# One merge-gate block placed earlier, three recurrence outputs placed before the scores, and one half-row add moved to GpSimd

## The chip, the cores and the metric

The kernel runs on one core of a Trainium2 chip. The metric is the device time in microseconds of one launch; for a kernel before and after a change, the medians of several runs are compared. All data is fp32. Where a matrix product is made, both operands are split into a high part in the type `float32r` and a low rest, and three products (high by high, low by high, high by low) are added up in PSUM, the accumulation memory of TensorE.

## The reference

One decoder layer over 512 tokens of width 1024. The input is normalised and projected once into ten pieces; two branches (block-sparse attention with 8 heads of 64, and a gated linear recurrence with 4 heads of 128) run beside each other; each is gated, projected up, and the two are merged by sigmoid gates; then come an output projection, a residual, and a gated input embedding.

```
xn = rmsnorm(h, norm_gain)
aq, ak, av, ag, bq, bf, bi, bg, gate_a, gate_b = split(xn @ w_in)
ya = moba_attention(rmsnorm(aq), rmsnorm(ak), av, rel_bias)      # 8 heads x 64
ya = (ya * silu(ag)) @ w_up_a
yb = hgrn2_chunkwise(silu(bq), kb(bf), bi, log_f(bf))            # 4 heads x 128
yb = (rmsnorm(yb) * silu(bg)) @ w_up_b
merged = sigmoid(gate_a) * ya + sigmoid(gate_b) * yb
h = h + merged @ w_out
h = h + (p @ w_ple) * sigmoid(h @ w_ple_gate)
```

## The kernel before

Everything after the first stage lies with features on the 128 partitions and the 512 tokens along the free axis. A dense block is one piece of 128 output features: 8 steps over the 1024 inputs, 3 matmuls of 128x512 in each, 24 in all, accumulated in one PSUM bank (`mm3`, L289 to L295). Banks come from three pools: `mm` with 3 (dense blocks, the fourth score bank of a run and the attention outputs), `a` with 3 (scores and recurrence outputs), `g` with 2 (diagonal blocks and states of the recurrence).

The order of TensorE is written out by hand. The main line goes through the list `ORDER` (L54 to L56): `bg` and `ag` are the output gates of recurrence and attention (`silu_block`, L486: three ScalarE instructions and a VectorE multiply, L491, that reads the bank last), `bf` stands for a head's forget and query blocks, `ga` and `gb` for the merge gates (`sigmoid`, L297: three ScalarE instructions, of which only the first reads the bank), `ub` for the recurrence's up-projection. Then follow the attention's up-projection (`ua`), the output projection (`h`, L1163) and the gated embedding (L1193 to L1279, product L1210, embedding `pe`).

Attention and recurrence are generators that are fed in between by a clock in the source: `mm3` and its kin call `tick` after each step of 3 matmuls, which adds the step's assumed time (0.681 us) to `now` and lets every generator run that is due; `cost` adds time without letting anybody run. What they issue on TensorE stands there, in that order, for good. The orders of VectorE and ScalarE and of the DMA queues are made by a planner from a simulated timeline, with the order of the source as priority; `high_priority` blocks go ahead. SyncE's queue (SP) issues most transfers, GpSimd's (POOL) the weights.

The attention (`attention`, L788) takes the head pairs 0 to 3 in two runs each: run 0 has the query blocks 0, 1, 2 and run 1 the query block 3 (`STEPS`). For each run it issues the scores on TensorE (L815), the bias, maximum, exponential and scaling (L832 to L836), transposes on VectorE (L839), and 16 transfers on SP that put the turned probabilities in their place (L850). The products with the values (`o`, L863) of a pair come behind the scores of the next pair's run 0; their last two fifths use run 1. After the scores of a run the generator sleeps for `PACE[run]`; of the sleep that ends in a run 0, the last 8 us (`BIAS`) begin with the transfers of the next bias (L880).

The recurrence (`hgrn_intra`, L529) makes decay products for a head, waits until the attention has issued its next run (`beside_attention`), and then puts small diagonal matmuls (`lpb`, `lpa`, L592 to L611) on TensorE. The output products of the head before (`hop`, L676 to L680, `cost(1.5)`) lie as a function in the list `hops` until then, and are issued in front of those matmuls (L583). Head 3's come by a clock of their own.

The end: for each of four pairs of output rows there are products in the gate, the embedding, and `merge` (L1181): sigmoid, multiply by the embedding (L1189), add of the residual (L1190, on VectorE where `n % 4 == 3`, on GpSimd elsewhere), and the store (L1191). Row 3 comes last, and its left half in two pieces of 128 tokens: `pe3l` and then `pe3m`.

Of the kernel before, what the change touches and what calls it, by code (L numbers as in the profile page):

```python
# [15 lines left out]
OP = mybir.AluOpType  # L16
# [12 lines left out]
LEVELS = (16, 8, 4, 2, 1)  # L29

STEPS = ((0, 1, 2), (3,))
PACE = (19.5, 22.5)

HP = 2.5
H0 = 8.0
# [16 lines left out]
XN = (0.6,) * 7 + (2.0, 0.6)  # L52

ORDER = [("bg", 0), ("ag", 0), ("bf", 1), ("bg", 1), ("ag", 1), ("gb", 0), ("bf", 2), ("gb", 1), ("gb", 2), ("bg", 2), ("ag", 2),  # L54
         ("gb", 3), ("bf", 3), ("gb", 4), ("gb", 5), ("bg", 3), ("ag", 3), ("ga", 0), ("ga", 1), ("gb", 6), ("gb", 7),
         ("ga", 4), ("ga", 2), ("ga", 3), ("ga", 5), ("ga", 6), ("ga", 7)] + [("ub", i) for i in range(KD)]  # L56

PAIRED = [n // 2 + 4 * (n % 2) for n in range(KD)]
# [10 lines left out]
def hybrid_layer_kernel(  # L69
# [17 lines left out]
    V, A, G, PE = nc.vector, nc.scalar, nc.gpsimd, nc.tensor  # L87
# [14 lines left out]
    def bank(tag, name):  # L102
        return psum.tile([128, 512], F32, tag=tag, bufs={"mm": 3, "g": 2, "a": 3}[tag], name=name)
# [34 lines left out]
    def cost(us):  # L138
        now[0] += us
# [18 lines left out]
    def held_from(us, insts, until=None):  # L158

        def later():  # L160
            for inst in insts if until not in done else []:
                held(inst)
            yield 0.0

        spawn(later(), us)
# [331 lines left out]
    hops = []  # L497
# [290 lines left out]
    def attention(qn, kn, va, sags, res):  # L788
        def place(qb, j):

            return {0: (j, 0), 1: (2, 256 * j), 2: (j, 128), 3: (j, 0)}[qb]

        def tiles(step):
            return 2 + (len(STEPS[step]) > 1)
# [3 lines left out]
        def scores(hp, step):  # L798
            (qh, ql), (kh, kl) = qn[hp], kn[hp]
            nt = tiles(step)  # L800

            sps = [bank("a", f"s{hp}{step}{i}") for i in range(nt)]
            extra = bank("mm", f"s{hp}{step}x") if nt > 2 else None

            def where(qb, j):
                b_, o = place(qb, j)
                return (extra, 0) if (qb, j) == (1, 1) else (sps[b_], o)

            for qb in STEPS[step]:
                nk = 128 * (qb + 1)  # L810
                for i in range(3):
                    for j in range(2):
                        js = slice(64 * j, 64 * j + 64)
                        b_, o = where(qb, j)
                        PE.matmul(b_[:, o:o + nk], (qh, ql, qh)[i][js, qb * 128:qb * 128 + 128], (kh, kh, kl)[i][js, :nk],  # L815
                                  start=(i == 0), stop=(i == 2))
            cost(sum(3 * max(0.107, (qb + 1) * 0.0538) for qb in STEPS[step]))
            return where

        def softmax(hp, step, T, where):  # L820

            nt = tiles(step)
            z = pb[:, Z0[step]:Z0[step] + nt].rearrange("p t f -> p (t f)").rearrange("p (b t f) -> p b t f", b=4, t=nt)
            with tc.high_priority(offset=AHEAD):
                left = [sum(place(qb, j)[0] == b for qb in STEPS[step] for j in range(2)) for b in range(nt)]
                for qb, j in [(qb, j) for qb in STEPS[step] for j in range(2)]:
                    b_, o = place(qb, j)
                    nk = 128 * (qb + 1)
                    p_ = pb[:, b_, o:o + nk]
                    st = unit("ps", f"ps{hp}{qb}{j}", shape=(128, 4))  # L830
                    s_, so = where(qb, j)
                    in_order(V.tensor_tensor_reduce(p_, s_[:, so:so + nk], T[j][:, nk - 1::-1], -1.0, 3e38,  # L832
                                                    OP.add, OP.min, st[:, 0:1]))
                    A.activation(p_, p_, AF.Exp, bias=st[:, 0:1], scale=-1.0, accum_out=st[:, 1:2])  # L834
                    V.reciprocal(st[:, 2:3], st[:, 1:2])
                    A.activation(p_, p_, AF.Copy, scale=st[:, 2:3])  # L836
                    left[b_] -= 1
                    if left[b_] == 0:
                        V.transpose(z[:, :, b_, :].rearrange("p b (n c) -> p b n c", c=32),  # L839
                                    pb[:, b_].rearrange("p (n b c) -> p b n c", b=4, c=32))  # L840
            return z

        def sorted_groups(step, z):

            nt = tiles(step)
            pt = pb[:, PT0[step]:PT0[step] + nt].rearrange("p t f -> p (t f)").rearrange("p (a t f) -> p a t f", a=4, t=nt)
            with tc.high_priority(offset=AHEAD):
                for a in range(4):
                    for b in range(4):
                        nc.sync.dma_start(pt[32 * b:32 * b + 32, a], z[32 * a:32 * a + 32, b])  # L850
            return pt.rearrange("p a t (n c) -> p a (t n) c", c=32)

        def out_values(hp, pts):

            o = bank("mm", f"o{hp}")
            for step, pt in enumerate(pts):
                for qb in STEPS[step]:
                    qs = slice(qb * 128, qb * 128 + 128)
                    for kb in range(qb + 1):
                        for j in range(2):  # L860
                            h0 = hp * 128 + 64 * j
                            b_, o0 = place(qb, j)
                            PE.matmul(o[64 * j:64 * j + 64, qs], va[kb][:, h0:h0 + 64], pt[:, :, 4 * b_ + o0 // 128 + kb, :],  # L863
                                      start=(kb == 0), stop=(kb == qb))
            cost(1.5)
            sag = sags[hp]
            V.tensor_tensor(sag, o, sag, op=OP.mult)
            h_ = unit("A", f"yah{hp}", R)
            l_ = unit("A", f"yal{hp}", R)
            split(h_, l_, sag)  # L870
            res.append((h_, l_))
            done.add(f"ya{hp}")
# [3 lines left out]
        def bias(hp):  # L876
            for j in range(2):
                t = unit("T", f"bias{hp}{j}")
                row = ed[2 * hp + j:2 * hp + j + 1, :]
                held(nc.sync.dma_start(t, bass.AP(tensor=row.tensor, offset=row.offset, ap=[[1, 128], [1, 512]])))  # L880
                T[hp, j] = t
# [10 lines left out]
        for n in range(len(steps) + 1):  # L892
            ahead = BIAS if 0 < n < len(steps) and steps[n][1] == 0 else 0.0
            if n >= 1:
                yield PACE[steps[n - 1][1]] - ahead
            if ahead:
                bias(steps[n][0])
                yield ahead
            if n < len(steps):
                hp, i = steps[n]  # L900
                where = scores(hp, i)
            if n >= 1 and steps[n - 1][1] == NS - 1:
                ho = steps[n - 1][0]
                while f"ag{ho}" not in done:
                    yield lambda: f"ag{ho}" in done
                out_values(ho, [pts.pop(n - NS + i_) for i_ in range(NS)])
            if n < len(steps):
                z = softmax(hp, i, [T[hp, 0], T[hp, 1]], where)
                if others:
                    parts.clear()  # L910
                    others.pop()()
                    for n_, p_ in enumerate(list(parts)):
                        held_from(16.0 + 2.0 * n_, [p_])
                pts[n] = sorted_groups(i, z)
            runs[0] += 1
# [84 lines left out]
    spawn(qk_norm("q", proj_tok(0, "aq", xh, xl), qgain[:, 0:1], qn))  # L1000
    spawn(qk_norm("k", proj_tok(1, "ak", xh, xl), kgain, kn))
    spawn(attention(qn, kn, va, sags, ya))
    def up(i, n, ys, name):
        ws = weight(w_up[n, i])
# [22 lines left out]
    for n in range(KD):  # L1027
        ga, gb = sg["ga", n], sg["gb", n]
# [11 lines left out]
    hf, xt, wt, edge = {}, {}, {}, []  # L1040
# [140 lines left out]
    def merge(n, c, ps, pes, t, plus=None):  # L1181
        if plus is not None:
            with tc.high_priority(offset=AHEAD):
                V.tensor_tensor(t[:, c], ps, plus, op=OP.add)  # L1184
            ps = t[:, c]
        if ps is not None:
            A.activation(t[:, c], ps, AF.Sigmoid)  # L1187
        yield
        V.tensor_tensor(t[:, c], t[:, c], pes()[:, c], op=OP.mult)  # L1189
        (V if n % 4 == 3 else G).tensor_tensor(t[:, c], t[:, c], hf[n][:, c], op=OP.add)  # L1190
        nc.sync.dma_start(out[n][:, c], t[:, c])  # L1191

    for p in range(4):  # L1193
# [152 lines left out]
```

## Time and profile before

| what | value |
|---|---|
| median of 3 runs | 451.46 us |
| lowest, highest | 451.43, 453.24 us |
| the profiled execution | 452.42 us |
| its span, first to last instruction | 450.6 us |
| granted TensorE clock, mean | 0.999 |
| DMA | 59.53 MB, mean 132 GB/s |

The profile comes from one execution, whose own time is 452.42 us: 1.8 us of that lie outside of the span. Times in the trace are microseconds from the start of the span. Engines are PE (TensorE matmuls), PEld (its weight loads), DVE (VectorE), ACT (ScalarE), POOL (GpSimd) and SP (SyncE); a small q marks an engine's queue of issued transfers. "[0.40 <-DVE bg3s L491]" behind a row means that the engine was idle for 0.40 us before it and that the instruction of line 491 which wrote `bg3s` ended the wait.

### The profile page before, as it was taken

What the parts mean: (1) busy time and instruction counts of PE and PEld (TensorE: products, weight loads), DVE (VectorE), ACT (ScalarE), POOL (GpSimd) and SP (SyncE); (2) the same over time, 40 slices, a digit from 0 to 9 for tenths busy, and PEclk for the clock granted to TensorE, in tenths of its full rate; (3) what the DMA queues carried; (4) which work ended last, traced back from release to release, by engine and by line L of the source; (5) the groups of instructions that cost most, each with busy time, mean ns of one, the idle gap of its engine ahead of it and who ended that gap; (6) DMA issues with size and microseconds to landing.
All of it is one profiled execution on the core that took longest, in us unless ns stands there. A gap on an engine that the chain in (4) does not pass through costs nothing.

```text
span 450.6 us, 8536 instructions
## 1 busy us (share of the span) xinstructions
PE 445.8 (99%) x3192; PEld 376.2 (83%) x3192; DVE 334.6 (74%) x682; ACT 289.7 (64%) x561; POOL 59.9 (13%) x97
## 2 busy tenths in 40 slices
PE   9999999999999999999999999999999999999996
PEld 8888888888878888878887888878888888899996
DVE  5869494776899797949857775465479868999844
ACT  5958474746689988979857996784135434555421
POOL 1000100000000101010100000111210103325520
PEclk9999999999999999999999999999999999999999
DMA  8802424168594455171425444265551444312111
GB/s 265 317 1 94 141 93 129 48 219 197 167 215 127 159 134 178 46 203 49 142 93 155 140 135 148 70 197 149 184 173 47 168 145 143 129 47 95 49 47 48
DMA packets 32857, 59.53 MB, mean 132 GB/s; under 512 B 7088, under 2 KB 18736, under 8 KB 32816
## 3 DMA queue, kind: packets, MB, share of 16 engines
q0 software_dynamic: 9056, 32.51, 22.5%
q1 hardware_dynamic: 23616, 26.47, 20.4%
q8 instruction: 25, 0.41, 0.4%
q14 instruction: 16, 0.13, 0.1%
q10 hardware_dynamic: 144, 0.01, 0.0%
HBM read 48.74 MB, written 4.98 MB: 119 GB/s over the span
## 4 chain that ended last, share of the span: by engine, by line
PE 89%; DVE 5%; SPq 2%; DMA 1%; issue 1%; ACT 0%; DVEq 0%
PE h L293 10%; PE g L1210 9%; PE ga L293 9%; PE gb L293 7%; PE ub L293 5%; PE aq L423 5%; PE ak L423 5%; PE ua L293 5%; PE av L423 5%; PE bf L293 5%; PE bi L423 5%; PE bq L293 4%; PE bg L293 4%; PE ag L293 4%; PE pe L293 2%; SPq L850 2%
## 5 line engine op out<-in xcount | busy, mean ns | idle before, releaser
L276 ACT ACTIVATE wh<-wf 128x1024 fp32r<-128x1024 f32 (+1 forms) x70 | 67.0, 958 | 63.2 <-issue 9.8
L277 DVE TENSOR_TENSOR wl<-wf,wh 128x1024 fp32r<-128x1024 f32 (+1 forms) x70 | 76.8, 1097 | 38.0 <-ACT wh L276 35.7
L266 POOL DMA_DIRECT2D wf<-in_w_tr_dram x30 | 15.8, 528 | 170.5 <-DVE wl L277 115.4
L293 PE MATMUL ga<-xh,wh 128*128 128x512 f32 x64 | 25.3, 396 | 0.4 <-DVE bg3s L491 0.4
L293 PE MATMUL gb<-xh,wh 128*128 128x512 f32 x64 | 25.0, 391 | 0.0
L293 PE MATMUL ga<-xh,wl 128*128 128x512 f32 x64 | 24.9, 390 | 0.0
L293 PE MATMUL ga<-xl,wh 128*128 128x512 f32 x64 | 24.9, 389 | 0.0
L293 PE MATMUL gb<-xl,wh 128*128 128x512 f32 x64 | 24.9, 389 | 0.0
L293 PE MATMUL h<-mh,wh 128*128 128x512 f32 x64 | 24.9, 389 | 0.0
L293 PE MATMUL h<-ml,wh 128*128 128x512 f32 x64 | 24.9, 389 | 0.0
L293 PE MATMUL h<-mh,wl 128*128 128x512 f32 x64 | 24.9, 389 | 0.0
L293 PE MATMUL gb<-xh,wl 128*128 128x512 f32 x64 | 24.9, 389 | 0.0
L834 ACT ACTIVATE pb<-pb,ps 128x128 f32<-128x128 f32 (+3 forms) x32 | 17.6, 551 | 10.0 <-DVE ps L832 10.0
L832 DVE CUSTOM_DVE_ANT_0 pb<-s,bias 128x128 f32<-128x128 f32 (+3 forms) x28 | 12.8, 493 | 7.1 <-DMA bias<-in_ed_dram 4.8
L1187 ACT ACTIVATE sg<-sg 128x256 f32<-128x256 f32 x12 | 5.0, 414 | 20.2 <-DVE sg L1184 20.2
L836 ACT ACTIVATE pb<-pb,ps 128x128 f32<-128x128 f32 (+3 forms) x32 | 16.0, 550 | 0.0
L542 ACT ACTIVATE hx<-hx 128x512 f32<-128x512 f32 x24 | 14.9, 623 | 1.4 <-DVE hx L541 1.3
L266 POOL DMA_DIRECT2D wf<-in_w_up_dram x16 | 8.6, 538 | 52.2 <-DVE wl L277 32.2
L839 DVE STREAM_TRANSPOSE pb<-pb 128x512 f32<-128x512 f32 x20 | 13.8, 696 | 2.0 <-ACT pb L836 2.0
L266 POOL DMA_DIRECT2D wf<-in_w_tok_dram x8 | 4.4, 549 | 80.2 <-DVE wl L277 68.2
L293 PEld LDWEIGHTS ga<-xh,wh 128*128 128x128 f32 x64 | 12.0, 188 | 3.5 <-DVE bg3s L491 0.8
L293 PEld LDWEIGHTS ga<-xh,wl 128*128 128x128 f32 x64 | 12.0, 188 | 2.6
(958 smaller groups left out, 1434.9 us busy)
## 6 DMA issues: line engine op xcount, KB each, us to landing
wf<-in_w_tr_dram POOLq DMA_DIRECT2D x30, 512.0 KB, 4.2
wf<-in_w_tok_dram POOLq DMA_DIRECT2D x8, 512.0 KB, 3.6
wf<-in_w_up_dram POOLq DMA_DIRECT2D x16, 256.0 KB, 3.0
wf<-in_w_o_dram POOLq DMA_DIRECT2D x8, 512.0 KB, 3.8
wf<-in_w_g_dram POOLq DMA_DIRECT2D x8, 512.0 KB, 3.6
wf<-in_w_tok_dram SPq DMA_DIRECT2D x6, 512.0 KB, 7.6
pb<-pb SPq DMA_DIRECT2D x64, 48.0 KB, 2.9
bias<-in_ed_dram SPq DMA_DIRECT2D x8, 256.0 KB, 4.1
```

What stands on the lines that cost most here:

```text
L266: (G if len(wraw) >= FAR else nc.sync).dma_start(raw, ap)
L276: rounds[i] = A.activation(hi, wraw[i], AF.Copy)
L277: V.tensor_tensor(lo, wraw[i], hi.bitcast(F32), op=OP.subtract)
L293: dense.append(PE.matmul(ps, a[:, k, :], b[k], start=(n == 0), stop=(n == tot - 1)))
L423: dense.append(PE.matmul(banks[t], a[:, s_], b[:, kk, :], start=(k == 0 and i == 0), stop=(k == KD - 1 and i == 2)))
L542: A.activation(x, x, AF.Exp)
L832: in_order(V.tensor_tensor_reduce(p_, s_[:, so:so + nk], T[j][:, nk - 1::-1], -1.0, 3e38, OP.add, OP.min, st[:, 0:1]))
L834: A.activation(p_, p_, AF.Exp, bias=st[:, 0:1], scale=-1.0, accum_out=st[:, 1:2])
L836: A.activation(p_, p_, AF.Copy, scale=st[:, 2:3])
L839: V.transpose(z[:, :, b_, :].rearrange("p b (n c) -> p b n c", c=32), pb[:, b_].rearrange("p (n b c) -> p b n c", b=4, c=32))
L850: nc.sync.dma_start(pt[32 * b:32 * b + 32, a], z[32 * a:32 * a + 32, b])
L1210: dense.append(PE.matmul(dst[i], a[:, k], b, start=(m == 0 and i in (1, 6, 5)), stop=(m == 11), skip_group_check=i not in (1, 6, 5)))
```

## The change

Three edits go to TensorE's order and its clock, one to the end.

- In `ORDER` the block `("ga", 0)` moves two places forward, ahead of `("bg", 3)` and `("ag", 3)`; the list of weight transfers is made from `ORDER` and moves with it.
- In the attention, when the run is number 1 and an output product of the recurrence waits in `hops`, it is issued there, in front of the scores. (The loop in `hgrn_intra` then finds the list empty.)
- `PACE[1]`, the sleep after run 1, goes from 22.5 to 21.0 us.
- In `merge` the add of the residual for the first 128 tokens of row 3 (`pe3l`) goes from VectorE to GpSimd; for row 7 no piece of that size exists.

```diff
-PACE = (19.5, 22.5)
+PACE = (19.5, 21.0)
...
-         ("gb", 3), ("bf", 3), ("gb", 4), ("gb", 5), ("bg", 3), ("ag", 3), ("ga", 0), ("ga", 1), ("gb", 6), ("gb", 7),
+         ("gb", 3), ("bf", 3), ("gb", 4), ("gb", 5), ("ga", 0), ("bg", 3), ("ag", 3), ("ga", 1), ("gb", 6), ("gb", 7),
...
                 hp, i = steps[n]
+                while i and hops:
+                    hops.pop()()
                 where = scores(hp, i)
...
-        (V if n % 4 == 3 else G).tensor_tensor(t[:, c], t[:, c], hf[n][:, c], op=OP.add)
+        (V if n % 4 == 3 and c != slice(0, 128) else G).tensor_tensor(t[:, c], t[:, c], hf[n][:, c], op=OP.add)
```

## The prediction

> **What bounds the kernel now.** I read the page's first part, then the waits of TensorE, then the chain of work that ended last, then the timeline around its one wait and at its end.
>
> ```profile
> PE 445.8 (99%) x3192; PEld 376.2 (83%) x3192; DVE 334.6 (74%) x682; ACT 289.7 (64%) x561; POOL 59.9 (13%) x97
> ```
>
> ```profile
> PE warm L193 <- PEq L1334: 0.8, 1, 0.8
> PE ga L293 <- DVE bg3s L491: 0.4, 1, 0.4
> ```
>
> ```profile
> 189.60 5.44 PE gb L293 x24
> ```
>
> ```profile
> 242.57 0.39 PE L293 MATMUL ga<-xh,wl 128*128 128x512 f32 x1
> 243.36 0.50 PE L293 MATMUL ga<-xh,wh 128*128 128x512 f32 x1 [0.40 <-DVE bg3s L491]
> ```
>
> TensorE is busy for 445.8 of 450.6 us. A busy PE need not be PE at its peak, but the chain shows a whole dense block, 24 matmuls, in 5.44 us, 0.227 us per matmul, and the other blocks are like it. TensorE waits only twice: 0.8 us at the start, and 0.4 us between ga0 and ga1. Matmul starts are normally 0.227 us apart; here they are 243.36 - 242.57 = 0.79 apart, so this wait costs 0.56 us. What remains, apart from it, is work that the change leaves alone, and the end behind the last matmul. So the change can win about 0.56 us and a few tenths at the end, and it can lose whatever new waits it makes on TensorE.
>
> Where the wait comes from is in the chain:
>
> ```profile
> 222.43 1.54 SPq L850
> ...
> 224.64 5.44 DMA bias<-in_ed_dram
> ...
> 230.21 0.29 DVE pb L832
> ...
> 242.70 0.61 DVE bg3s L491
> ...
> 243.36 5.74 PE ga L293 x24
> ```
>
> The 16 transfers of pair 1's run 1 fill SP until 224; only then is the bias of pair 2 issued, the second half lands 5.44 us later, VectorE stands at L832 until 230.21, and works off its backlog until L491 has read the bank of bg3 at 243.31. The `mm` pool has three banks: bg3, the fourth score bank s20x and the output o1 hold them; ag3 and ga0 take those of s20x and o1, and ga1 has to have bg3's.
>
> **The change part by part.** *Merge-gate block first (expected gain 0.56 us).* The same blocks run, in the order ga0, bg3, ag3, ga1. Now ga1 gets the bank that ga0 leaves, and bg3's is wanted one block (5.44 us) later, by gb6. ga0's bank is free after its first ScalarE instruction, not after a chain of four.
>
> ```profile
> 238.69 0.57 ACT L298 ACTIVATE bg3s<-bg 128x512 f32<-128x512 f32 x1
> ```
>
> ```profile
> 230.77 0.42 DVE L832 CUSTOM_DVE_ANT_0 pb<-s20x,bias 128x256 f32<-128x256 f32 x1
> ```
>
> ```profile
> 231.89 0.40 PE L293 MATMUL ag<-xh,wh 128*128 128x512 f32 x1
> ```
>
> At the same place bg3's first ScalarE instruction ran at 238.69 to 239.26; ga1 starts at about 231.89 + 2 x 5.44 = 242.8 without the wait. If ga0's takes that place, 3.5 us are left. It isn't of high priority as bg3's is, so this cover isn't certain. The three instructions of ga0 come 5.44 us earlier or more, those of bg3 and ag3 later; their number is the same. gb6 wants bg3's bank at 248.2; VectorE had cleared its backlog by 243.31 in the old run, so 5 us or so are there. The next block after the values now wants s20x's bank: bg3 instead of ag3, at the same 231.89 and with the same 231.19 (230.77 + 0.42) before it: 0.7 us of slack, no gain, no loss, unless L832 comes later. Weight transfers move with their blocks, same sizes, two blocks ahead; POOL is busy for 13% and issues them as before. I take 0.56 gained; the ends are 0.56 gained and 0 (the wait changes its owner).
>
> *Outputs before the scores, and the sleep 1.5 us shorter (expected 0).* These two belong together. In run 1 of pairs 0 to 2 the order was scores, hop, lpb:
>
> ```profile
> 152.56 0.90 PE s L815 x6
> 153.46 0.64 PE hop L678 x4
> ...
> 155.22 0.36 PE lpb L592 x16
> ```
>
> One hop takes 155.22 - 153.46 = 1.76 us, the scores 0.90. Afterwards it is hop, scores, lpb: the scores come 1.76 us later, the hop 0.90 earlier, lpb stays. The clock in the source decides what follows. Before, after the scores the generator slept 22.5 us, in which the hop's cost of 1.5 and lpb's 1.2 passed with no dense work; waking needs 2.7 + 0.681 k >= 14.5, so k = 18, and 8 us later k = 30. Now the hop's 1.5 lies ahead of the sleep: 1.2 + 0.681 k >= 13.0 gives k = 18 again, and then k = 30. So the 30 steps between the runs stay exactly 30, and the next run's scores, the bias issue and `o` stay where they are on TensorE. Only behind pair 3 there is no hop to offset: 22.5 / 0.681 takes 34 steps, 21.0 takes 31, so o3 moves 3 steps (2.04 us) forward, from 323.52 to about 321.5.
>
> ```profile
> 323.52 2.33 PE o L863 x40
> ...
> 329.52 0.68 PE ua L293 x3
> ```
>
> Its result is wanted at 329.52 and TensorE doesn't wait there, so 2 us more cover are worth nothing. Its last turned transfers are issued until 305.83 + 10.03 = 315.86, which leaves 5.6 us for the landing:
>
> ```profile
> 305.83 10.03 SPq L850 DMA_DIRECT2D pb<-pb  x16
> ```
>
> What can cost is that the softmax of runs 1 starts 1.76 us later while its consumers stay. Two places are near:
>
> ```profile
> 153.46:165.83 12.37, 12.37 (x183) 10.66 (x184) 12.37 (x31) 12.13 (x28) 0.53 (x1) 1.00 0.53 142
> 202.53:212.96 10.43, 10.43 (x175) 8.95 (x174) 10.43 (x28) 10.35 (x24) 0.53 (x1) 1.00 0.17 54
> ```
>
> ```profile
> 165.87 10.75 SPq L850 DMA_DIRECT2D pb<-pb  x16
> ```
>
> ```profile
> pb<-pb SPq DMA_DIRECT2D x1, 32.0 KB, 2.9
> ```
>
> ```profile
> 178.59 2.33 PE o L863 x40
> ```
>
> (The windows give each engine's busy time: PE, PEld, DVE, ACT, POOL. They go from the end of the scores, or the first L832, to the end of the second transpose L839.) First place: the transfers of pair 0 are issued from 165.87, the last at 176.03, landing 2.9 later at 178.94; `o` uses them in its last 16 of 40 matmuls, from 178.59 + 24 x 0.058 = 180.0. Slack: 1.05 us. Second place: pair 1's transfers hold the bias, so a delay d there delays L832 and with it s20x's bank, where 0.7 us are free. Does d become 1.76? VectorE is busy for 12.37 of 12.37 and 10.43 of 10.43 us between the scores and the transposes, ScalarE for 12.13 and 10.35: the transposes come when the queue's work is done, not when the scores' own chain (two L832 of 0.68, then ScalarE) is. The hop's part of that work (L695, L313, L315) is ready 0.90 us earlier and can fill the time that the scores leave. So the bounds are 0 (only the order within a full queue changes) and 1.76 (the planner shifts all with the scores); a little below 0 can't be excluded, since the hop's work might go ahead of the stretch, but it would win nothing on TensorE. By the rows nearest to it, full queues, I take d between 0 and 0.7, hence no wait: 0.
>
> *Half-row add on GpSimd (expected 0).*
>
> ```profile
> 446.43 0.29 DVE L1189 TENSOR_TENSOR sg<-sg,pe3l 128x128 f32<-128x128 f32 x1 [0.28 <-PE pe3l L293]
> 446.75 0.29 DVE L1190 TENSOR_TENSOR sg<-sg,hf 128x128 f32<-128x128 f32 x1
> 447.04 0.29 DVE L1189 TENSOR_TENSOR sg<-sg,pe3m 128x128 f32<-128x128 f32 x1
> 447.36 0.29 DVE L1190 TENSOR_TENSOR sg<-sg,hf 128x128 f32<-128x128 f32 x1
> ```
>
> ```profile
> 446.72 0.28 PE L293 MATMUL pe3m<-ph,pwl 128*128 128x128 f32 x1
> ```
>
> ```profile
> 423.08 1.29 POOL L1067 TENSOR_TENSOR pb<-wf,wf 128x512 f32<-128x512 f32 x1 [1.37 <-DVE w32l L1052]
> 424.33 1.19 POOL L1190 TENSOR_TENSOR sg<-sg,hf 128x256 f32<-128x256 f32 x1
> ...
> 436.24 0.73 POOL L1190 TENSOR_TENSOR sg<-sg,hf 128x256 f32<-128x256 f32 x1 [1.97 <-DVE sg L1189]
> ```
>
> ```profile
> 447.11 0.90 SPq L1191 DMA_DIRECT2D out_dram<-sg  x2
> ```
>
> VectorE loses one add of 0.29 us between two multiplies. But the second multiply can't start before pe3m's last matmul ends at 447.00, and it starts at 447.04 already. So the gain is between 0 and 0.29, nearest to 0.04. GpSimd's add: 128x512 took 1.29 and 128x256 0.73, so 128x128 is an estimate of 0.73 - 0.28 = 0.45 us; from about 446.8 to 447.25. Its store is issued at about 447.3 instead of 447.11, and SP is free for the last one about 0.4 later, at the old 447.68. Cost 0. If the add takes as long as the row at 424.33 has for twice the size (1.19, beside a busy VectorE; half of it is 0.6), its store goes out at 447.4, and the last one 0.1 late; at the full 1.19, 0.7 late.
>
> ```profile
> 413.79 0.68 DVE L1068 TENSOR_TENSOR pb<-wf,pb 128x512 f32<-128x512 f32 x1
> ```
>
> ```profile
> 424.17 0.75 DVE L1061 TENSOR_TENSOR pb<-pb,wf 128x512 f32<-128x512 f32 x1
> 424.95 1.12 DVE L1068 TENSOR_TENSOR pb<-wf,pb 128x512 f32<-128x512 f32 x1
> ```
>
> When both engines add from SBUF at once, both are slow here: GpSimd's row of 424.33 takes 1.19 instead of 0.73, VectorE's L1068 beside it 1.12 instead of 0.68. The Trainium skill, "SBUF — State Buffer", section Who interferes with whom, has the rule: a VectorE instruction with two SBUF inputs and a GpSimd instruction that reads SBUF contend for one read interface, one with at most one SBUF input doesn't. The trace agrees. At the end the add on GpSimd lies beside the multiply L1189, which reads one input from PSUM, and VectorE's last add would begin at 447.36, after 447.25; the two meet only if GpSimd's add is late by more than 0.1 us.
>
> **The sum.** -0.56 + 0 + 0 = -0.56 on the span, 450.6 to 450.0; the profiled execution's 452.42 would be 451.9. The median of the runs, 451.46, lies 0.96 below the profiled execution; I take the difference to it: 451.46 - 0.5 = **450.95 us**, with 0.06 left for the small shifts. That is 0.1%, and a measurement of this kernel can tell about 0.5% (2.26 us) from no change.
>
> **The rivals.**
> - *The lateness isn't absorbed (slower).* For: the transposes hang on the scores, and the slacks of 1.05 and 0.7 us are below 1.76. Against: the full queues. With d = 1.76, o0 waits 0.71 us, bg3 waits 1.06 for s20x's bank, the gain stays 0.56: +1.21, 452.65. It decides from d = 0.7 on, and the net is a loss from about d = 1.2. VectorE would then stand longer at L832, and the weights' low halves, made behind it, could add a wait; that could bring it to 453.
> - *The wait changes its owner (no change).* ga1 then waits for ga0's ScalarE instruction, or gb6 for bg3: about 451.4. For: the instruction isn't of high priority, and even bg3's, which is, ran 6.8 us behind its block (231.89 to 238.69). Against: 3.5 and 5 us of slack.
> - *The two engines meet at the end.* GpSimd's add reaches into VectorE's last one; by the rows of 1.19 against 0.73 each waits for the other's 0.46 at most: 450.95 + 0.46 = 451.4. For: only 0.1 us lies between them. Against: the estimate of 0.45. It would follow from the port rule of the Trainium skill's "SBUF — State Buffer" named above.
>
> **How the numbers follow.** Forecast (450.4 to 451.3): 0.60. Lateness: 0.22, from 451.6 to 453.7, of which 0.04 lie beyond 453.72. Owner: 0.09. End: 0.07. The rest, 0.02, is a queue order that I don't foresee. The two middle cases fall into the range of the forecast's upper end; the lateness case is taken in as far as 452.8. Range 450.2 to 452.8: below it about 0.04, above it about 0.09. Faster than 449.20 would need 2.26 us, and only 0.56 and 0.29 are there: 0.01. Slower than 453.72: 0.05. Within: 0.94.
>
> **What would show it.** Right: TensorE's waits list no ga behind bg3s, ga1 starts 0.23 us after ga0's last matmul, the order hop, s, lpb at three places, o3 at about 321.0 with the half microsecond gained, the last transposes of runs 1 at about the old times. Wrong: a wait of `o` on the turned transfers, of bg3 on L832, of ga1 on ScalarE, or a last store later behind the last matmul than 447.68 - 447.00 = 0.68 us.

## The result, and the profile after

The changed kernel takes **456.34 us** (median of 6 runs, 455.93 to 456.76) against 451.82 us of the kernel before on the same chip: a ratio of **1.0095, interval 1.0080 to 1.0111**. (A ratio, here and below, is worked out from the single runs of both kernels and can differ by up to 0.2% from the quotient of the two medians.) It is slower by about 0.95%, where 450.95 us had been forecast and the range ended at 452.8. The profiled execution took 456.76 us, its span is 455.0 us (before: 452.42 and 450.6). Behind L898 the lines of the changed kernel stand two further down: the multiply is L1191, the add L1192, the store L1193, the program's closing L1343.

The first part of the page after, and TensorE's whole list of waits (us in total, times, longest):

```profile
PE 446.1 (98%) x3192; PEld 377.1 (83%) x3192; DVE 334.4 (74%) x681; ACT 290.1 (64%) x561; POOL 60.8 (13%) x98
```

```profile
PE warm L193 <- PEq L1336: 0.8, 1, 0.8
PE o L863 <- DMA pb<-pb: 0.8, 2, 0.5
```

TensorE is busy for 446.1 us, 0.3 more than before, and waits for 0.8 instead of 0.4 us besides the start. Its last matmul ended at 447.00 before and ends at 447.63 now. So of the 4.3 us that the span grew (450.62 to 454.96), 0.6 lie ahead of the last matmul and 3.7 behind it: 454.96 - 447.63 = 7.3 us against 450.62 - 447.00 = 3.6. Of the 0.6, 0.4 were there before any edit takes effect: TensorE's block aq starts at 60.31 instead of 59.93.

The timeline of the end, on VectorE, then on GpSimd:

```profile
447.07 0.29 DVE L1191 TENSOR_TENSOR sg<-sg,pe3l 128x128 f32<-128x128 f32 x1 [0.29 <-PE pe3l L293]
447.67 0.29 DVE L1191 TENSOR_TENSOR sg<-sg,pe3m 128x128 f32<-128x128 f32 x1 [0.31 <-PE pe3m L293]
447.99 0.29 DVE L1192 TENSOR_TENSOR sg<-sg,hf 128x128 f32<-128x128 f32 x1
```

```profile
447.49 0.45 POOL L1192 TENSOR_TENSOR sg<-sg,hf 128x128 f32<-128x128 f32 x1 [9.88 <-DVE sg L1191]
```

The work itself ends as forecast: GpSimd's add takes 0.45 us and ends at 447.94, VectorE's last add ends at 448.28, and the last store goes out at 448.39, 0.76 us behind the last matmul (before: 0.68). It lands at 450.00. The span ends 5 us after that. What stands there is in the instructions of the closing line, L1343 after and L1341 before (engine, operation, count, duration in ns as min/median/max, first and last start):

```profile
L1343 SPq EVENT_SEMAPHORE  x11: 17/28/28, 448.8 to 454.9; - x11
...
L1343 POOLq DRAIN  x3: 40/241/6289, 447.5 to 454.7; - x3
```

```profile
L1341 POOLq DRAIN  x3: 40/93/6577, 436.2 to 450.1; - x3
```

Behind the last instruction that the program gives it, GpSimd's queue runs a DRAIN; its row begins just ahead of that instruction's and ends behind it. After, it starts at 447.46, takes 6.29 us and ends at 453.75, which is **5.81 us behind the end of GpSimd's add**; SP's next semaphore comes at 453.92, and 1.2 us after the DRAIN the span ends. Before, the same DRAIN started at 436.20, took 6.58 us and ended at 442.78, again 5.81 us behind the last add (436.24 + 0.73), but 6.5 us ahead of the last store's landing at 449.24. It cost nothing there, and a sequencer's DRAIN counts in no engine's busy time. The change put one GpSimd instruction into the last microsecond of the work, and so the whole DRAIN behind it.

### The profile page after: what moved, and what is told of

It is laid out like the page before. It is cut to its first block, busy times and chain, and to the rows that moved or that the text cites. A ratio compares the mean times of both kernels' runs of the same rounds, so it can differ in the third digit from the quotient of the medians.

```text
span 455.0 us, 8534 instructions
## 1 busy us (share of the span) xinstructions
PE 446.1 (98%) x3192; PEld 377.1 (83%) x3192; DVE 334.4 (74%) x681; ACT 290.1 (64%) x561; POOL 60.8 (13%) x98
## 4 chain that ended last, share of the span: by engine, by line
PE 87%; SPq 4%; DVE 3%; ACT 2%; DMA 2%; issue 1%; DVEq 0%
PE h L293 10%; PE g L1212 9%; PE ga L293 9%; PE gb L293 5%; PE ub L293 5%; PE aq L423 5%; PE ak L423 5%; PE ag L293 5%; PE ua L293 5%; PE av L423 5%; PE bf L293 5%; PE bi L423 4%; SPq L850 4%; PE bg L293 4%; PE bq L293 3%; PE pe L293 2%
## 5 line engine op out<-in xcount | busy, mean ns | idle before, releaser
L266 POOL DMA_DIRECT2D wf<-in_w_tr_dram x30 | 15.9, 530 | 170.7 <-DVE wl L277 135.0
L266 POOL DMA_DIRECT2D wf<-in_w_up_dram x16 | 8.6, 540 | 54.6 <-DVE wl L277 40.8
L266 POOL DMA_DIRECT2D wf<-in_w_tok_dram x8 | 4.4, 552 | 80.5 <-DVE wl L277 68.5
L293 PEld LDWEIGHTS gb<-xh,wh 128*128 128x128 f32 x64 | 12.0, 188 | 2.5
```

The source lines that it names most:

```text
L266: (G if len(wraw) >= FAR else nc.sync).dma_start(raw, ap)
L293: dense.append(PE.matmul(ps, a[:, k, :], b[k], start=(n == 0), stop=(n == tot - 1)))
```

## The experiments: which part costs

The first four kernels ran on one chip, with the same runs of the kernel before (452.10 us, 29 runs).

**The change without the half-row add on GpSimd.**

```diff
-        (V if n % 4 == 3 and c != slice(0, 128) else G).tensor_tensor(...)
+        (V if n % 4 == 3 else G).tensor_tensor(...)
```

> The changed kernel with the add of the residual for row 3's first 128 tokens back on VectorE; all else as changed. Theory 1 (the end): after its last arithmetic GpSimd's closing drain takes 5.8 us, and the program's end waits for it; with the last GpSimd add back at about 437 the drain is hidden. Then the time falls by 3.7 us against the changed kernel, to about 452.6, which is 0.8 over before. Rival (the late transfers and the new queue orders of the attention cost it all): the time stays at 456.3.

452.43 us, ratio 1.0008 (0.9998 to 1.0018). The DRAIN starts at 436.21 again. The loss is gone.

**The half-row add alone**, in the kernel before.

```diff
-        (V if n % 4 == 3 else G).tensor_tensor(...)
+        (V if n % 4 == 3 and c != slice(0, 128) else G).tensor_tensor(...)
```

> The kernel before with the GpSimd add alone. Theory 1: slower by 3.6 to 3.9 us, about 455.6, with a drain on GpSimd's queue that ends 5.8 us after the add, and TensorE's end unchanged at 447.0. Rival (the add only delays a store or shares a read port): slower by 0.1 to 0.5 us.

455.86 us, ratio 1.0079 (1.0065 to 1.0094), with the DRAIN at the end:

```profile
L1341 POOLq DRAIN  x3: 40/241/6289, 447.2 to 454.4; - x3
```

So one half-row add of 0.45 us makes the loss, alone or with the rest.

**The gate block alone.**

```diff
-         ("gb", 3), ("bf", 3), ("gb", 4), ("gb", 5), ("bg", 3), ("ag", 3), ("ga", 0), ("ga", 1), ("gb", 6), ("gb", 7),
+         ("gb", 3), ("bf", 3), ("gb", 4), ("gb", 5), ("ga", 0), ("bg", 3), ("ag", 3), ("ga", 1), ("gb", 6), ("gb", 7),
```

> The kernel before with the merge gate's block moved alone. If the step of the prediction holds: TensorE's wait behind bg3s is gone and nothing takes its place; faster by 0.6 to 0.9 us (the gap of 0.56 and a slow restart of the matmuls behind it), about 451.0. Rival (the wait changes its owner): 451.8.

452.11 us, ratio 1.0004 (0.9991 to 1.0017). The wait of ga1 is gone from the list, but the 0.56 us, which would be 0.9988, are not to be seen in the time.

**Recurrence outputs and sleep alone.**

```diff
-PACE = (19.5, 22.5)
+PACE = (19.5, 21.0)
...
+                while i and hops:
+                    hops.pop()()
```

> The kernel before with outputs before scores and the shorter sleep, nothing else. Theory 2: the turned transfers come too late for o in pairs 0 and 1, TensorE waits some 0.7 and 0.5 us there, and the wait at ga1 stays or shrinks as the bias is no longer late: slower by 0.3 to 1.2 us, 452.1 to 453.0. Rival (these waits came from the moved gate block): no wait at o, 451.8.

451.86 us, ratio 0.9998 (0.9988 to 1.0007). TensorE waits for the turned transfers at o0 and o1, as in the whole change, if for less:

```profile
PE warm L193 <- PEq L1336: 0.8, 1, 0.8
PE o L863 <- DMA pb<-pb: 0.5, 2, 0.3
```

The wait of ga1 is gone here too, although the gate block stands in its old place: the bias of pair 2 is now issued at 201.63, ahead of pair 1's last 16 transfers, and not behind them at 224.01. By this profile the gate block has no wait left to remove in the whole change.

**Recurrence outputs and gate block, with the old sleep of 22.5** (against the changed kernel):

```diff
-PACE = (19.5, 21.0)
+PACE = (19.5, 22.5)
...
-        (V if n % 4 == 3 and c != slice(0, 128) else G).tensor_tensor(...)
+        (V if n % 4 == 3 else G).tensor_tensor(...)
```

> The block of the gate and the recurrence outputs as in the changed kernel, but the sleep left at 22.5 and row 3's half-row add left on VectorE, so the output products stand three steps of TensorE (3 x 0.68 = 2.04 us) later than in the changed kernel. Theory 1: the waits of 0.7 and 0.5 us at o0 and o1 come from the shorter sleep, because the turned scores are late by less than these 2.04 us: only TensorE's first wait (0.8, warm) is left in its list, no start-to-start gap over 0.25 us stands at o0 and o1, and the time is 0 to 0.2% under that of the kernel before (ratio 0.998 to 1.000). Rival 1: the waits come from the outputs in front of the scores, which hold VectorE and ScalarE by more than 2.04 us: a wait at o0 or o1 stays in the list. GpSimd's closing DRAIN begins by 436.5 and ends by 443.5.

453.90 us against 452.62, ratio 1.0039 (1.0017 to 1.0060), with 12 runs spread from 451.5 to 457.2. At o0 no wait is left, as theory 1 had it; at o1 one stays, which is the rival's sign; and neither had the two other waits of the list:

```profile
PE lpa L563 <- issue: 1.4, 1, 1.4
PE warm L193 <- PEq L1336: 0.8, 1, 0.8
PE o L863 <- DMA pb<-pb: 0.4, 1, 0.4
PE bf L293 <- DVE bg1s L491: 0.4, 1, 0.4
```

A stall of 1.4 us shows up in the middle of lpa's matmuls, for which the profile shows no releaser. The DRAIN begins at 437.5 and has nothing to do with it. What the stall is stays open; as a repair of the waits at o the longer sleep is no good.

## The experiments: what the DRAIN waits for

**Is it the add, or any late GpSimd instruction?** In the kernel before, and each by itself: a small memset on GpSimd behind the last use of row 3's first 128 tokens; row 3's right half-row add on GpSimd; the last but one store issued by GpSimd's queue.

```diff
+        if n == 3 and c == slice(0, 128):
+            G.memset(hf[n][:, c], 0.0)
```

> The kernel before, and a GpSimd memset of 128x128 that clears row 3's residual after its last use, at about 447.1; all adds stay where they were, the output is the same. If GpSimd's drain takes 5.8 us after whatever arithmetic comes last: slower by 3.3 to 3.7 us (the memset is shorter than the add by 0.25). If only a two-input add that reads SBUF leaves something to drain: no change, 452.1, with a drain of under 0.3 us behind the memset.

```diff
+        (V if n % 4 == 3 and (n, c) != (3, rh) else G).tensor_tensor(...)
```

> The kernel before, with the add for the right half of row 3 (256 tokens) on GpSimd instead; it runs at about 445.8 to 446.5, 1.4 us ahead of the add of the change. If the end is the later of the stores' end and (GpSimd's last end + 5.8 us): the drain ends at 452.3 and the kernel is slower by 2.2 to 2.6 us, about 454.5. If a late GpSimd add costs a fixed price: 3.7 slower, 455.8. If the price comes from sharing the port at the very end: no change.

```diff
+        (G if n == 3 and c == slice(0, 128) else nc.sync).dma_start(...)
```

> The kernel before, with the store of row 3's first 128 tokens issued by GpSimd's queue instead of SP's; no late arithmetic on GpSimd. If the drain waits for transfers of GpSimd's queue, or follows whatever GpSimd does last: slower by 3 to 6 us. If it follows arithmetic alone: within 0.7 us of before (an issue of 0.53 us and a landing of about 2 us).

Against 452.38 us of the kernel before they took 455.61 (ratio 1.0092, 1.0061 to 1.0123), 455.99 (1.0081, 1.0052 to 1.0110) and 457.62 us (1.0117, 1.0089 to 1.0145). GpSimd's last instruction and the DRAIN, in the memset's kernel:

```profile
446.37 0.20 POOL L1192 MEMSET hf<- 128x128 f32 x1 [10.13 <-DVE sg L1190]
```

```profile
L1343 POOLq DRAIN  x3: 102/174/6031, 446.4 to 453.2; - x3
```

The memset ends at 446.57, the DRAIN (446.35 + 6.03) at 452.38: 5.81 us again. The same two rows of the kernel with the right half-row add, then of the kernel with the store:

```profile
446.01 0.73 POOL L1190 TENSOR_TENSOR sg<-sg,hf 128x256 f32<-128x256 f32 x1 [8.85 <-DVE sg L1189]
```

```profile
L1341 POOLq DRAIN  x3: 40/241/6567, 446.0 to 453.5; - x3
```

```profile
446.94 0.58 POOL L1191 DMA_DIRECT2D out_dram<-sg  x1 [10.66 <-DVE sg L1189]
```

```profile
L1341 POOLq DRAIN  x3: 40/93/6484, 446.9 to 454.2; - x3
```

Behind the add of twice the size it is 5.81, behind the DMA's issue 5.87. Neither the operation nor its length matters, only when GpSimd's last instruction ends.

The time of the right half-row add doesn't show this by itself: a loss of 2.2 to 2.6 us was expected if the end of the add decides and 3.7 with a fixed price. Its ratio is 3.7 us, with an interval from 2.4 to 5.0 that barely reaches the first. Its profile does show it: the span ends 6.57 us behind the last matmul, where the late half-row add alone has 7.32. A fixed price would have made the two equal; the add ends 0.44 us ahead of the last matmul in the one and 0.31 behind it in the other, which is the same 0.75.

**From where on does it cost?** Two adds of row 7 moved to GpSimd, one that starts at 441.24 on VectorE, one at 444.70.

```diff
+        (V if n % 4 == 3 and (n, c) != (7, rh) else G).tensor_tensor(...)
```

> The kernel before, with the add for the right half of row 7 (256 tokens) on GpSimd; it runs at about 441.3 to 442.0. By the rule of 5.8 us its drain ends at 447.8, before the last store lands at 449.2: no change, 452.1. If a GpSimd add in the last pair costs in any place: 2 to 4 us slower.

453.06 us, ratio 1.0015 (1.0002 to 1.0028). In its profile the add ends at 441.09 and the DRAIN at 446.90, ahead of the last store's landing at 448.25; the span ends 3.7 us behind the last matmul (before: 3.6). The 0.15% is not to be found in this profile, whose execution was the fastest of the ten.

```diff
+        (V if n % 4 == 3 and (n, c) != (7, lh) else G).tensor_tensor(...)
```

> The kernel before, with only row 7's left half-row add moved from VectorE, where it starts at 444.70, to GpSimd. Theory 1 (GpSimd's closing DRAIN ends 5.81 us after its last instruction, and the program's end waits for it): the add ends at about 445.4, the DRAIN at about 451.2, some 2.0 us after the last store's landing in the profile before (449.24); so the span grows by some 1.9 us to about 452.5, less than half of what the late add of row 3 cost, and the ratio is 1.003 to 1.005. Rival 1 (any GpSimd work near the end costs the same 3.5 us and more, or nothing below a threshold): ratio over 1.007, or within 0.001 of 1.

454.36 us against 452.62, ratio 1.0037 (1.0023 to 1.0051), half of what the latest add costs, as the theory gave it.

```profile
445.90 0.74 POOL L1190 TENSOR_TENSOR sg<-sg,hf 128x256 f32<-128x256 f32 x1 [7.36 <-DVE sg L1189]
```

```profile
L1341 POOLq DRAIN  x3: 40/235/6572, 445.9 to 453.4; - x3
```

The DRAIN ends at 445.88 + 6.57 = 452.45, 1.6 us behind the last store's landing at 450.81, and the span ends 1.5 us further behind the last matmul than before (5.1 against 3.6). The rule of this kernel: GpSimd's last instruction has to end some 5.8 us before the last store lands.

**Can the DRAIN be paid earlier?** DRAINs put in front of row 1's stores gave no answer, since the planner, seeing no operands, put them at the program's start:

```diff
+        if n == 1:
+            G.drain()
         nc.sync.dma_start(out[n][:, c], t[:, c])
```

> The kernel before, with a DRAIN of GpSimd put in front of each of row 1's two stores, some 40 to 60 us before the end (the output is the same). Theory 1 (a DRAIN takes some 5.8 us behind the last instruction wherever GpSimd has worked): each of these rows lasts 5.8 us and more, and GpSimd's next add starts that much later. Rival 1 (only the closing DRAIN takes so long; the one at the start took 0.19 us): each lasts under 1.5 us. In both the closing DRAIN stays hidden and the time is within 0.5% of before.

```profile
L1192 POOLq DRAIN  x2: 401/560/719, 0.8 to 1.7; - x2
```

They end 0.07 us behind the GpSimd instruction beside them. Time 452.80 us against 452.62, 1.0006 (0.9995 to 1.0018). So a DRAIN isn't long as such. The next kernel holds two of them in the order of the source, ahead of row 2's stores, together with the late add:

```diff
+        (V if n % 4 == 3 and c != slice(0, 128) else G).tensor_tensor(...)
+        if n == 2:
+            tc.keep_in_program_order(G.drain())
```

> The kernel before with the half-row add on GpSimd as in the change, and in front of each of row 2's two stores (around 425 to 436 us) a DRAIN of GpSimd, held behind the GpSimd work written ahead of it. Two questions. First, what a DRAIN within the program lasts: theory 1 (it is a price of the DRAIN itself once GpSimd has worked for long) says that it ends some 5.8 us behind the last GpSimd instruction ahead of it; rival 1 (the price belongs to the closing of the program) says that it ends within 0.1 us of it, as the DRAINs at the program's start did. Second, what an earlier DRAIN leaves for the closing one: theory 1a (the price is paid at each DRAIN) and rival 1 say that the closing one still ends 5.81 us after the late add and the ratio stays at 1.007 to 1.010; theory 1b (a DRAIN clears something that has gathered, once) says that the closing one ends within 0.1 us and the ratio falls to 0.999 to 1.002.

452.69 us against 452.74, ratio 1.0003 (0.9984 to 1.0023). The DRAINs of row 2, GpSimd's last instructions, and the closing DRAIN:

```profile
L1192 POOLq DRAIN  x2: 2156/4372/6589, 429.1 to 436.0; - x2
```

```profile
429.18 0.74 POOL L1190 TENSOR_TENSOR sg<-sg,hf 128x256 f32<-128x256 f32 x1 [4.31 <-DVE sg L1189]
435.97 2.14 POOL L1190 TENSOR_TENSOR sg<-sg,hf 128x256 f32<-128x256 f32 x3 [6.05 <-DVE sg L1189]
446.20 0.45 POOL L1190 TENSOR_TENSOR sg<-sg,hf 128x128 f32<-128x128 f32 x1 [8.10 <-DVE sg L1189]
```

```profile
L1343 POOLq DRAIN  x3: 34/102/547, 446.2 to 450.0; - x3
```

The first DRAIN ends at 435.73, 5.81 us behind its add (429.18 + 0.74). The second, behind three adds, ends 0.07 us behind the last of them, and so does the closing one behind the late add. The price is paid **once**, for something that has gathered up to the first DRAIN, and the late add then costs nothing that the time shows.

**The whole change with these two DRAINs.**

```diff
         (V if n % 4 == 3 and c != slice(0, 128) else G).tensor_tensor(...)
+        if n == 2:
+            tc.keep_in_program_order(G.drain())
```

> The whole change, with a DRAIN of GpSimd in front of each of row 2's two stores. Theory 1b (the closing DRAIN's 5.8 us is work that has gathered and that an earlier DRAIN takes away): the closing DRAIN ends within 0.1 us of the late add, the ratio to the kernel before falls from 1.0095 to between 0.997 and 1.002, and what is left of the change (gate block, recurrence outputs, sleep) is seen by itself. Rival (the other parts of the change cost as well, by the waits at o0 and o1): ratio over 1.002.

452.99 us against 452.18, ratio 1.0017 (1.0000 to 1.0033), where the change had 1.0095. The closing DRAIN, behind the late add:

```profile
L1345 POOLq DRAIN  x3: 34/102/547, 447.4 to 451.2; - x3
```

That gives back nearly all of the loss and shows that the DRAIN was its cause; whether the rest of the change is neutral or costs 0.1 or 0.2% can't be told. No version that was run beats the kernel before.

**What gathers?** GpSimd issues 70 loads (L266) in the course of the program. The next kernel has the two DRAINs, and then one more DMA issued by GpSimd as its last instruction.

```diff
+        if n == 2:
+            tc.keep_in_program_order(G.drain())
-        nc.sync.dma_start(out[n][:, c], t[:, c])
+        (G if n == 3 and c == slice(0, 128) else nc.sync).dma_start(out[n][:, c], t[:, c])
```

> The kernel before, with the two DRAINs of GpSimd in front of row 2's stores, and the last but one store (row 3, first 128 tokens) issued by GpSimd's queue instead of SP's. What had gathered before the DRAIN of 5.8 us? Theory G1 (the DMAs that GpSimd issues; the last of its loads is issued at 403.9): with one more DMA issued at about 447 the closing DRAIN ends some 5.8 us behind it again, and the span is 3 us longer than before. Rival G2 (the adds and products of the whole program, or something that is done only once): the closing DRAIN ends within 0.2 us of the DMA's issue and the time is within 0.3% of before.

```profile
447.33 0.58 POOL L1193 DMA_DIRECT2D out_dram<-sg  x1 [8.90 <-DVE sg L1190]
```

```profile
L1343 POOLq DRAIN  x3: 34/147/2077, 447.3 to 450.8; - x3
```

The DMA's issue ends at 447.91, the closing DRAIN at 449.38, 1.47 us behind it, and only 0.08 behind the landing of that DMA at 449.30. 453.08 us against 452.18, ratio 1.0017 (1.0002 to 1.0033). One DMA doesn't bring the 5.8 us back, so neither theory held as it was put. Then DRAINs behind the 10th and the 30th load, in the kernel before:

```diff
             (G if len(wraw) >= FAR else nc.sync).dma_start(raw, ap)
+            if len(wraw) in (FAR + 9, FAR + 29):
+                tc.keep_in_program_order(G.drain())
```

> The kernel before, with a DRAIN of GpSimd behind its 10th load and one behind its 30th (GpSimd issues 70 loads in all); 40 loads are then left for the closing DRAIN. So far: behind 70 loads it ended 5.81 us after GpSimd's last instruction, behind 71 DMAs 5.88, behind one 1.47, behind none 0.07. Theory L (it grows with the number of DMAs issued since the last DRAIN: 1.40 for the first and (5.74 - 1.40)/69 = 0.063 for each more, added to 0.07): 10 loads give 2.0 us, 20 give 2.7, 40 give 3.9. Rival S (a fixed price of 5.8 once the loads of the program have begun, whatever their number): the DRAIN behind the 10th and each later one take about 5.8. The time itself may change a little, since the DRAINs hold back loads.

```profile
L268 POOLq DRAIN  x2: 4017/5066/6114, 91.6 to 219.1; - x2
```

```profile
435.65 0.74 POOL L1192 TENSOR_TENSOR sg<-sg,hf 128x256 f32<-128x256 f32 x1 [1.96 <-DVE sg L1191]
```

```profile
L1343 POOLq DRAIN  x3: 46/102/4111, 435.6 to 449.8; - x3
```

452.20 us against 451.99, ratio 1.0001 (0.9973 to 1.0029). With 40 loads since the last DRAIN, the closing one (435.62 + 4.11) ends 3.34 us behind the add; with 70 it was 5.81, with none 0.07. That is a line: (5.81 - 3.34) / 30 = 0.082 us for each load, and 0.07 + 40 x 0.082 = 3.35; for the 71 DMAs of the kernel with the late store it gives 5.89, where 5.87 was measured.

Two other ways to count fit worse: by bytes (the 40 loads bring 16 of the 31 MB) the closing DRAIN would end 3.0 us behind the add, by the time since the last DRAIN (210 of 436 us) 2.8. GpSimd's arithmetic can't be what went: but for the program's start, all of it lies behind the second DRAIN. Each of these loads writes 128 rows, so a price for a load and one for a row aren't told apart.

The fixed price falls; my 1.40 for the first DMA falls too, since the DRAIN of the kernel with one DMA had waited for its landing. The two DRAINs within this run had the same wait: they end 3.47 us (10 loads) and 5.57 us (20 loads) behind the issue of the load just before them, but only 0.46 and 0.86 us behind its landing, at 95.13 and 224.35. Counted from the landing those two are shorter than the line gives (0.89 and 1.71), and how the wait and the price for each load join stays open. What the DRAIN does for a load isn't shown either.

## Why the prediction was wrong, step by step

- **Half-row add on GpSimd (expected 0): this step failed.** What it worked out held to 0.1 us: the add took the estimated 0.45 us, its store left at once, the two engines didn't meet in a way that cost (VectorE's last add took 0.29 us as before). But the step asked only what the add does to the store, not what GpSimd still has to do behind its last instruction. The DRAIN of 6.58 us at 436.2 stood in the trace before, in the instructions of the closing line; the busy shares and the chain to the last store, on which the step rests, show none of it. Its condition could have been worked out: 447.25 + 5.81 = 453.1 for the DRAIN's end, against a last landing at 449.24, so some +3.8 us, and 456.2 instead of 452.42 for the profiled execution; the add alone took 456.48 in its profiled execution, 455.86 in the median. No rival of the list was this one; it was the 0.02 of "a queue order that I don't foresee".
- **Gate block first (expected 0.56 us): right in mechanism, wrong in size.** The wait of ga1 behind bg3s is gone, and ga1 starts at 244.25, 0.23 us behind the last matmul of ag3. (The prediction's sign names ga0 there, but by the new order ag3 is the block ahead of ga1.) But the wait was that of a few executions, not of the kernel. Seven profiles share TensorE's order up to the end (before, and the runs that moved only GpSimd work at the end); it stands in two of them, with 0.4 and 0.3 us, and in the others it doesn't, nor in the four with DRAINs added to the kernel before. In the profile of before the second half of the bias landed at 230.07, in the memset's kernel at 228.21, and there L491 was done 1.9 us earlier. How late an execution itself runs at that place counts as well: in the kernel with row 3's right half-row add, the bias landed at 230.24, and TensorE, later by some tenths there, didn't wait. A wait of half a microsecond that hangs on a landing needs more than one execution before it is counted as a gain.
- **Outputs before the scores, shorter sleep (expected 0): right in the time, wrong in the waits.** The 30 steps between the runs stayed, and o3 moved from 323.52 to 322.11 in an execution whose last matmul ran 0.63 us late, which makes the 2.04 of three steps. The delay d was put between 0 and 0.7:

```profile
155.58 0.75 DVE L695 SCALAR_TENSOR_TENSOR bg0s<-hop,sm,bg0s 128x512 f32<-128x512 f32 x1 [0.41 <-ACT ho L692]
156.25 0.68 DVE L832 CUSTOM_DVE_ANT_0 pb<-s,bias 128x512 f32<-128x512 f32 x1
...
156.85 0.71 DVE L313 STREAM_TRANSPOSE hy<-ho 128x512 f32<-128x512 f32 x1
157.48 0.65 DVE L832 CUSTOM_DVE_ANT_0 pb<-s,bias 128x512 f32<-128x512 f32 x1
```

```profile
166.97 11.00 SPq L850 DMA_DIRECT2D pb<-pb  x16
...
200.98 4.86 SPq L880 DMA_DIRECT2D bias<-in_ed_dram  x2
216.16 10.80 SPq L850 DMA_DIRECT2D pb<-pb  x16
```

```profile
180.94 1.09 PE L863 MATMUL o<-pb,avv 128*64 128x128 f32 x16 [0.49 <-DMA pb<-pb]
```

The planner put the hop's work around the scores' own on VectorE, with an idle 0.41 us ahead of it, so the queue was not as full as the argument had it. Pair 0's turned transfers are issued from 166.97 instead of 165.87; 0.38 of these 1.10 us is this execution's later start, so d is 0.7. For pair 1 they are issued 3.17 us later (216.16 against 212.99), of which 2 to 3 us are d, outside my bounds. There the bias of pair 2 is now issued ahead of the transfers (200.98), so the delay reaches nobody but o1.

The slack of 1.05 us at o0 wasn't enough, as the first rival had it: starts stand 0.71 us further apart than their length at o0 and 0.49 at o1. That the rival's own figure for o0 is 0.71 too is luck: it came from d = 1.76 and a landing 2.9 us behind the issue, and here d is 0.7 and the landing took 3.5.

In the three other kernels with these outputs and the shorter sleep it is 0.33, 0.42 and 0.20 us at o0 and 0.32, 0.53 and 0.11 at o1 (without the add, without add and gate block, with the DRAINs). The profile of the DRAINs at the program's start has 0.90 us at o0 with the outputs in their old place: the last transfer was issued at 175.99, as before, but took 4.5 us to land. So the landing decides there as much as the issue. In the time, these waits are within what the run without the add leaves, 1.0008 (0.9998 to 1.0018).

- **What would show it wrong** named a wait of `o` on the turned transfers, which came, as told above, and a last store later behind the last matmul than 0.68 us. It came 0.76 behind, which is next to nothing; the number that would have shown the loss is the distance from the last matmul to the end of the span, 3.6 before and 7.3 after.

## What to carry to other kernels

Read the end of a program to the end of its span, on every queue, and not only to the last store: what an engine runs behind its last instruction is hidden as long as that instruction is early. Before giving an idle engine a last small job, add what its closing takes to the job's end and compare that with the last landing; here an engine that is busy for 13% was the wrong one for 0.45 us of work in the last 6 us. Where GpSimd has issued many DMAs and must work to the end, a DRAIN put into an idle stretch of it earlier takes the price over (1.0079 became 1.0003).

## What the runs showed of the hardware

- GpSimd's DRAIN ends 0.07 us behind its last instruction when it has issued no DMA since the last DRAIN, 3.34 us behind 40 loads and 5.81 behind 70: some 0.08 us for each of these loads of 128 rows. It is the same behind an add, a memset and an add of another size; at the program's start a DRAIN takes 0.19 us with the memsets ahead of it.
- With a DMA of GpSimd's queue still on its way, the DRAIN ends behind that DMA's landing (0.08 us with one DMA, 0.46 with ten, 0.86 with twenty).
- The same transfer, the last of pair 0's 16 in run 1, landed 1.8 us behind its issue in the memset's kernel, 2.9 in the kernel before and 4.5 in the one with DRAINs at the program's start.
- The same order of TensorE doesn't give the same waits in each execution: over the kernels that differ only in GpSimd work at the end, one wait of 0.4 us came and went, and others of 0.7 and 0.8 us, at bi and bf, stood in one execution alone (that with row 7's left half-row add).
